# Grouped-query attention with its scores transposed, in an encoder layer on one core

## The chip, the cores and the metric

The kernel runs on one core of a Trainium2 chip. The metric is the device time of one execution in microseconds (us). Engines are named as in the profile: PE is TensorE (matrix products; PEld is its loading of weights), DVE is VectorE, ACT is ScalarE, POOL is GpSimd, SP is SyncE, which issues most DMAs. PSUM is the memory that products are written to; a bank of it holds 128 x 512 float32.

## The reference

One layer over 512 tokens of width 1024: `z = x @ w_in` is split into neighbourhood attention (8 heads of 64), grouped-query attention (8 query heads and 2 key/value heads of 64), attention into 256 memory tokens, and three gates; the branches are projected, gated, summed and normalised; then come 16 experts. What the change touches is this part:

```
q = apply_rope(rms_norm(q, q_gain), cos, sin)        # 8 query heads
k = apply_rope(rms_norm(k, k_gain), cos, sin)        # 2 key heads, 4 query heads to each
s = einsum('bkgqd,bskd->bkgqs', q, k) / sqrt(64)     # per head: 512 queries x 512 keys
p = softmax(s, axis=-1)                              # over the keys
y = einsum('bkgqs,bskd->bqkgd', p, v)
```

## The kernel before

Weights come as 74 units of 128 x 1024 over SP's queue. Each unit is split by `hi_lo` into a rounded high part (ACT) and the rest (DVE), and a product of two tensors is made as three products of such parts. A unit is split two pieces of work ahead of its use.

The program is written out by hand in the order in which each engine runs it. The mixers run as a generator that issues a piece of PE work (a gate: 24 products of 128x512; a projection, or half of a block of the neighbourhood values: 12) and yields. At each yield `run` calls one step of an attention (`at.step`) and then one background stage from `bg` (rotary of q and k). So a step of attention stands between two pieces of PE work, in one queue per engine.

Three generators concern us. `g_branch(2)` is the memory branch: 8 gates and 8 projections, 16 yields. `g_na_v` makes the neighbourhood values: 8 yields. `g_na_qk(0)` makes the first neighbourhood queries and keys: 2 yields. After them comes `g_branch(1)`, which needs the result of the grouped-query attention (`y1`).

The grouped-query attention is 16 units, each a pair of heads `hp` (0 to 3) and a block `m` of 128 queries. `S` makes the scores of two heads with queries in PSUM's partitions (two products a head: key high part and key rest, each against query high and rest stacked in 128 rows). `soft` takes the maximum per query (DVE), the exponential with its sum (ACT), and `norm` multiplies by 1/sum (DVE). One step later `T` transposes the probabilities on PE (8 products of 128x128), `tev` copies them to SBUF (one copy on DVE, one on ACT), and for two blocks together `PV` makes the values (16 float32 products with 64-column weights). `run(g_branch(2, True), 1.0, 4)` makes the first step at the fifth yield.

PSUM has eight banks here: three called `mm` for the pieces, `S0` and `S1`, `T0` and `T1`, and `Y`. `PB("S")` and `PB("T")` hand out the two banks of a kind in turn. A product into a bank waits until the bank's last reader is done.

Of the kernel before, what the change touches and what calls it, by code (L numbers as in the profile page):

```python
# [18 lines left out]
P = 128  # L19
# [28 lines left out]
HOMES = {30: "E0", 31: "A5", 32: "A6", 33: "bf", N_UNITS - 1: "A7"}  # L48
# [44 lines left out]
def layer_kernel(ctx: ExitStack, tc: tile.TileContext, xt, xn, first0, wu, bgate, rpb, gains, wrt,  # L93
# [299 lines left out]
    def rope_stages(q, zs, nh, which):  # L393
# [47 lines left out]
        def sk(g):  # L441
            if not kT:
                kT.append(heads_T(0))
            src = kT[0][g * 64:g * 64 + 64]
            for o in (0, 64):
                nc.scalar.copy(khh[o:o + 64, g], src)
            for o in (0, 64):
                nc.vector.tensor_tensor(klo[o:o + 64, g], src, khh[o:o + 64, g].bitcast(F32), op=ALU.subtract)

        def sq_(pair):  # L450
            hp = 2 * (q - 1) + pair
# [14 lines left out]
    def g_gqa():  # L466
# [4 lines left out]
                  rope=(R("VS", [P, 1024], "ropesq"), b1t[:, 1]), zr=R("B0", [P, 2, 1024], "ropeout"))  # L471
# [170 lines left out]
    class GqaUnit:  # L642
        GROUP = 2

        def __init__(self, hp, m):
            self.hp, self.m = hp, m

        def S(self):
            self.s = []
            for h in range(2):  # L650
                g = self.hp // 2
                tok = slice(self.m * P, (self.m + 1) * P)
                q = ST["qs"][g][:, 2 * (self.hp % 2) + h, tok]
                s = PB("S", f"gs{self.hp}{self.m}{h}")
                nc.tensor.matmul(s, q, ST["khh"][:, g], start=True, stop=False)
                nc.tensor.matmul(s, q, ST["klo"][:, g], start=False, stop=True)
                self.s.append(s)

        def soft(self):
            self.p = twin("P").rearrange("p (h c) -> p h c", h=2)  # L660
            self.sm = small([P, 2], "sm")
            nm = small([P, 2], "nm")
            for h in range(2):
                nc.vector.tensor_reduce(nm[:, h:h + 1], self.s[h], axis=AX.X, op=ALU.max, negate=True)  # L664
                nc.scalar.activation(self.p[:, h], self.s[h], AF.Exp, bias=nm[:, h:h + 1],  # L665
                                     accum_out=self.sm[:, h:h + 1])

        def norm(self):
            recip_norm(self.p, self.sm, lambda h: self.p[:, h])

        def T(self):
            self.t = []
            for h in range(2):
                t = PB("T", f"gt{self.hp}{self.m}{h}", (P, 4, P))
                for kc in range(4):
                    nc.tensor.transpose(t[:, kc], self.p[:, h, kc * P:(kc + 1) * P], ident)  # L676
                self.t.append(t)

        def tev(self):
            self.pt = twin("PT").rearrange("p (h k c) -> p h k c", h=2, k=4)  # L680
            nc.vector.tensor_copy(self.pt[:, 0], self.t[0])
            nc.scalar.copy(self.pt[:, 1], self.t[1])

        def PV(self, group):

            self.y = PB("Y", f"gy{self.hp}{self.m}")
            kvh = self.hp // 2
            for j, u in enumerate(group):
                for kc in range(4):
                    for h in range(2):  # L690
                        nc.tensor.matmul(self.y[h * 64:h * 64 + 64, j * P:(j + 1) * P],  # L691
                                         ST["vg"][:, kc, kvh * 64:kvh * 64 + 64], u.pt[:, h, kc],
                                         start=(kc == 0), stop=(kc == 3))

        def yev(self, group):
            yh, yl = ST["y1"]
            n = len(group) * P
# [1224 lines left out]
```

## Time and profile before

| | |
|---|---|
| median of 3 runs | 935.5 us (934.7 to 935.88) |
| the profiled execution's own time | 935.11 us |
| its span on the core | 933.3 us (1.8 us lie around it) |
| PE busy | 917.4 us (98%) |
| DVE, ACT, POOL busy | 451.6, 280.9, 72.3 us |

Busy is time in which the engine has an instruction at work. PE's products overlap, so the distance between starts tells what one costs, not its duration. A stage is read from the time by engine within it.

### The profile page before, as it was taken

How to read it: one execution, taken by the hardware profiler on the slowest of the kernel's cores; microseconds unless marked ns; L12 is line 12 of the kernel's file. 1: busy time of each engine (PE TensorE's matmuls, PEld its weight loads, DVE VectorE, ACT ScalarE, POOL GpSimd, SP SyncE). 2: the span in 40 equal slices, each digit the busy share in tenths (PEclk: the TensorE clock that was granted, in tenths of full speed). 3: DMA queues.
4: the chain of work that ended last, by engine and by line, in shares of the span. 5: the costliest groups of instructions: out<-in, count | busy, mean ns of one | idle time of the engine just before them, and what ended most of it. 6: DMA issues, size and time to landing. Idle time of an engine off the chain costs nothing.

```text
span 933.3 us, 13429 instructions
## 1 busy us (share of the span) xinstructions
PE 917.4 (98%) x5497; PEld 604.2 (65%) x5497; DVE 451.6 (48%) x859; ACT 280.9 (30%) x573; POOL 72.3 (8%) x107
## 2 busy tenths in 40 slices
PE   9999999999999999999999999999999999999996
PEld 8899988888888888888787344434343444533332
DVE  6448869875375566326545147223141323422245
ACT  6334443644344454334333011101011010301021
POOL 0000000000132230107023000000000000000001
PEclk9999999999999999999999999999999999999998
DMA  9322221222333332474878999999999999999997
GB/s 366 100 73 66 87 70 46 69 69 68 96 83 113 105 89 72 177 279 179 316 316 354 412 424 433 426 438 429 436 435 429 426 428 431 428 433 428 430 425 291
DMA packets 40012, 251.42 MB, mean 269 GB/s; under 512 B 12720, under 2 KB 13264, under 8 KB 24592
## 3 DMA queue, kind: packets, MB, share of 16 engines
q1 hardware_dynamic: 39728, 250.22, 66.9%
q8 instruction: 43, 0.70, 0.3%
q0 software_dynamic: 80, 0.26, 0.1%
q14 instruction: 17, 0.14, 0.0%
q10 hardware_dynamic: 144, 0.10, 0.0%
HBM read 247.42 MB, written 2.36 MB: 268 GB/s over the span
## 4 chain that ended last, share of the span: by engine, by line
PE 77%; DMA 16%; DVE 4%; ACT 1%; issue 0%; SPq 0%; POOLq 0%; DVEq 0%; ACTq 0%
DMA gu<-in_wst 15%; PE g L1386 7%; PE u L1386 7%; PE y L1447 6%; PE gate L306 5%; PE gate L308 4%; PE gate L307 4%; PE pr L306 2%; PE pr L307 2%; PE pr L308 2%; PE ga L1350 2%; PE gy L691 2%; PE nqk L306 2%; PE nqk L307 2%; PE nqk L308 2%; PE gt L676 1%
## 5 line engine op out<-in xcount | busy, mean ns | idle before, releaser
L1386 PE MATMUL g<-gu,xs 128*64 128x512 f32 x408 | 106.1, 598 | 0.8 <-DMA gu<-in_wst 0.7
L1386 PE MATMUL u<-gu,xs 128*64 128x512 f32 x408 | 104.9, 592 | 0.0
L1447 PE MATMUL y<-dn,hT 128*64 128x512 f32 x376 | 83.6, 593 | 0.9 <-DMA dn<-in_wst 0.8
L150 DVE TENSOR_TENSOR y<-y,y 64x512 fp32r<-64x512 f32 x28 | 19.3, 689 | 120.2 <-ACT y L149 120.2
L150 DVE TENSOR_TENSOR lo_twin<-raw_twin,whi 128x1024 fp32r<-128x1024 f32 x40 | 49.0, 1226 | 46.2 <-ACT whi L149 46.1
L149 ACT CAST y<-y 64x512 fp32r<-64x512 f32 x28 | 16.2, 580 | 174.1 <-PE y L1447 146.6
L1386 PEld LDWEIGHTS u<-gu,xs 128*64 128x64 f32 x408 | 29.4, 137 | 58.1 <-issue 57.6
L149 ACT CAST whi<-raw_twin 128x1024 fp32r<-128x1024 f32 x60 | 63.0, 1050 | 12.1 <-PE wo L1159 9.4
L1447 PEld LDWEIGHTS y<-dn,hT 128*64 128x64 f32 x376 | 27.0, 137 | 54.5 <-issue 51.5
L1386 PEld LDWEIGHTS g<-gu,xs 128*64 128x64 f32 x408 | 26.8, 137 | 46.2 <-issue 40.0
L1429 DVE COPY hT<-ht 128x512 f32<-128x512 f32 x15 | 10.4, 692 | 61.5 <-PE ht L1426 61.4
L306 PE MATMUL gate<-xha,whi 128*128 128x512 f32 x96 | 38.7, 403 | 0.0
L307 PE MATMUL gate<-xla,whi 128*128 128x512 f32 x96 | 37.4, 390 | 0.0
L306 PE MATMUL gate<-xhb,whi 128*128 128x512 f32 x96 | 37.3, 389 | 0.0
L307 PE MATMUL gate<-xlb,whi 128*128 128x512 f32 x96 | 37.3, 389 | 0.0
L712 POOL TENSOR_TENSOR bm<-bf,hm 128x256 f32<-128x256 f32 x24 | 18.9, 827 | 236.7 <-DMA bf<-in_rpb 232.9
L1535 DVE TENSOR_TENSOR acc<-acc,cb 128x512 f32<-128x512 f32 x56 | 34.0, 680 | 3.7 <-PE cb L1533 3.7
L1350 PEld LDWEIGHTS <-x 128*128 128x128 f16 (+1 forms) x576 | 29.7, 100 | 9.0 <-issue 8.7
L665 ACT ACTIVATE P_twin<-gs,nm 128x512 f32<-128x512 f32 x32 | 21.7, 684 | 42.8 <-DVE nm L664 42.8
L1410 DVE SCALAR_TENSOR_TENSOR h<-h,g 128x512 f32<-128x512 f32 x15 | 10.3, 688 | 49.5 <-ACT h L1409 49.5
L150 DVE TENSOR_TENSOR wlo<-raw_twin,whi 128x1024 fp32r<-128x1024 f32 x20 | 24.5, 1226 | 17.9 <-ACT whi L149 17.9
L308 PE MATMUL gate<-xha,lo_twin 128*128 128x512 f32 x80 | 31.2, 391 | 0.0
(489 smaller groups left out, 1998.7 us busy)
## 6 DMA issues: line engine op xcount, KB each, us to landing
gu<-in_wst SPq DMA_DIRECT2D x31, 2048.0 KB
gu<-in_wst SPq DMA_DIRECT2D x45, 1024.0 KB
raw_twin<-in_wu SPq DMA_DIRECT2D x65, 512.0 KB
dn<-in_wst SPq DMA_DIRECT2D x14, 2048.0 KB
dn<-in_wst SPq DMA_DIRECT2D x18, 1024.0 KB
gu<-in_wst SPq DMA_DIRECT2D x4, 4096.0 KB
dn<-in_wst SPq DMA_DIRECT2D x4, 4096.0 KB
gu<-in_wst SPq DMA_DIRECT2D x2, 3072.0 KB
```

The costliest lines, as they stand in the source:

```text
L149: nc.scalar.copy(hi, src)
L150: nc.vector.tensor_tensor(lo, src, hi.bitcast(F32), op=ALU.subtract)
L306: nc.tensor.matmul(acc, w_h, rh[:, k], start=(k == 0), stop=False)
L307: nc.tensor.matmul(acc, w_h, rl[:, k], start=False, stop=False)
L308: nc.tensor.matmul(acc, w_l, rh[:, k], start=False, stop=(k == nk - 1))
L665: nc.scalar.activation(self.p[:, h], self.s[h], AF.Exp, bias=nm[:, h:h + 1], accum_out=self.sm[:, h:h + 1])
L691: nc.tensor.matmul(self.y[h * 64:h * 64 + 64, j * P:(j + 1) * P], ST["vg"][:, kc, kvh * 64:kvh * 64 + 64], u.pt[:, h, kc], start=(kc == 0) ...
L712: nc.gpsimd.tensor_tensor(bm[:, h, ty].rearrange("p (b r c) -> p r b c", b=4, r=8), bf[:, h, :, 16 - 8 * ty:48 - 8 * ty].rearrange("p r (b ...
L1350: nc.tensor.matmul(g[r], part(i, m)[:, f * P + r.start:f * P + r.stop], oh[:, m], start=(i == 0 and m == 0), stop=(i == 1 and m == NT - 1))
L1386: nc.tensor.matmul(GU[e][b][hf * 64:hf * 64 + 64], xs, w[b][:, hf * 512:hf * 512 + 512], start=(k == 0), stop=(k == KD - 1))
L1447: nc.tensor.matmul(ys[o][o * 64:o * 64 + 64], hT[:, c, hf * 64:hf * 64 + 64], w[j][:, o * 512:(o + 1) * 512], start=(first and k == 0 and ...
L1535: nc.vector.tensor_tensor(a, a, cb, op=ALU.add)
```

## The change

`GqaFlow` takes the place of the 16 units. The scores are made with keys in the partitions, so that the probabilities need no transposing. The maximum per query must then be known first. `peak` makes approximate scores from the high parts alone (64 rows, queries in the partitions), and DVE takes their negative maxima. `rows` transposes them on PE into 4 rows and writes those into the moving operand of the second product, against four weight rows of ones. `scores` then gives scores less maximum, and ACT's exponential needs no bias. The sums over keys are made on POOL (`add`), then by a product with ones (`divide`); the reciprocal and the multiplication follow the values, on 128x512 per pair of heads. The query heads come in the order 0, 2, 1, 3. A step is now one pair of heads and one block of 128 keys. The start is one yield later, and steps go on at the yields of `g_na_qk(0)`; what is left runs in `gqa.drain()`. The table rows of the first neighbourhood bias are loaded at the same place as before, and POOL's additions to them follow the drain. One unit's home moves from `E0` to `VS`, and two of four DVE subtractions for the key's rest go.

```diff
+            lead = [[lambda m=m: self.peak(0, m, 0, "T"), lambda m=m: self.peak(0, m, 1, "S")] for m in range(NT)]
+            lead[0] += [lambda: self.high(0), lambda: self.high(2)]
+            self.steps += lead
+            self.steps.append([lambda: self.rows(0)])
+            todo = [(hp, kc) for hp in (0, 2, 1, 3) for kc in range(NT)]
+            for i in range(len(todo) + 3):
+                f = []
+                if 2 <= i < 6:
+                    f.append(lambda m=i - 2: self.peak(1, m, 0, "T"))
+                if i < len(todo):
+                    f.append(lambda u=todo[i], i=i: self.scores(u, i))
+                if i == 7:
+                    f.append(lambda: self.rows(1))
+                if 0 < i <= len(todo):
+                    f.append(lambda u=todo[i - 1], i=i - 1: self.values(u, i))
+                if 2 <= i < 6:
+                    f.append(lambda m=i - 2: self.peak(1, m, 1, "T"))
+                if i < len(todo):
+                    f.append(lambda u=todo[i], i=i: self.add(u, i))
...
+                if i >= 5 and (i - 5) % NT == 0 and i - 5 < len(todo):
+                    f.insert(0, lambda hp=todo[i - 5][0]: self.divide(hp))
+                self.steps.append(f)
...
+        def peak(self, j, m, h, tag):
...
+            for g in range(2):
+                o = 64 * g
+                s = PB(tag, f"gm{j}{m}{h}{g}")
+                nc.tensor.matmul(s, self.q(j + 2 * g, h)[o:o + 64, m * P:(m + 1) * P], ST["khh"][o:o + 64, g],
+                                 start=True, stop=True)
+                ss.append(s)
+            for g in range(2):
+                nc.vector.tensor_reduce(self.nm[j][:, m, g, h:h + 1], ss[g], axis=AX.X, op=ALU.max, negate=True)
...
+        def scores(self, u, i):
+            hp, kc = u
+            g, c = hp // 2, slice(kc * P, kc * P + P)
+            ss = [PB("S", f"gs{hp}{kc}{h}") for h in range(2)]
             for h in range(2):
+                nc.tensor.matmul(ss[h], ST["khh"][:, g, c], self.q(hp, h), start=True, stop=False)
             for h in range(2):
+                nc.tensor.matmul(ss[h], ST["klo"][:, g, c], self.slot(hp, h), start=False, stop=True)
+            for h in range(2):
+                nc.scalar.activation(self.pt[i % 4][:, h * S:h * S + S], ss[h], AF.Exp)
...
+                nc.gpsimd.tensor_tensor(self.acc[hp][h], old, self.pt[i % 4][:, c], op=ALU.add)
...
+            for h in range(2):
+                nc.tensor.matmul(self.y[h * 64:h * 64 + 64], v, self.pt[i % 4][:, h * S:h * S + S],
+                                 start=(kc == 0), stop=(kc == NT - 1))
+            if kc == NT - 1:
+                nc.scalar.copy(ST["gtmp"][:, S:], self.y)
+
+        def divide(self, hp):
+            rc, y = ST["gtmp"][:, :S], ST["gtmp"][:, S:]
+            sm = PB("T", f"gd{hp}")
+            for h in range(2):
+                nc.tensor.matmul(sm[h * 64:h * 64 + 64], self.ones, self.acc[hp][h], start=True, stop=True)
+            nc.vector.reciprocal(rc, sm)
+            nc.vector.tensor_tensor(y, y, rc, op=ALU.mult)
+            yh, yl = (t[:, hp] for t in ST["y1"])
+            nc.scalar.copy(yh, y)
+            nc.gpsimd.tensor_tensor(yl, y, yh.bitcast(F32), op=ALU.subtract)
...
-    run(g_branch(2, True), 1.0, 4)
-    run(g_na_v(), 1.0)
-    at.drain()
-    na_bias(0)
-    run(g_na_qk(0))
+    gqa = GqaFlow()
+    run(g_branch(2, True), 1.0, 5, gqa)
+    run(g_na_v(), 1.0, 0, gqa)
+    bf0 = na_rows(0)
+    run(g_na_qk(0), 1.0, 0, gqa)
+    gqa.drain()
+    na_bias(0, bf0)
```

Three places in the order of instructions show what stands where. In the names, `gs`, `gm`, `gy`, `gd` and `gt` are PSUM tiles (scores, approximate scores, values, sums, transposed probabilities) and the last number of a name only tells buffers apart.

The first place is behind the last projection of `g_branch(2)`, PE's order. Before, it held the scores of a unit, the values of two blocks and the transposes of the unit ahead:

```order
L655 MATMUL gs230_2008<-kk_557,qs1_560 128x512
L656 MATMUL gs230_2008<-kk_557,qs1_560 128x512
L655 MATMUL gs231_2011<-kk_557,qs1_560 128x512
L656 MATMUL gs231_2011<-kk_557,qs1_560 128x512
L691 MATMUL gy20_2014<-PT_twin_681,vgt_558 64x128 x16
L676 MATMUL gt220_2031<-ident_137,P_twin_627 128x128 x4
L676 MATMUL gt221_2036<-ident_137,P_twin_627 128x128 x4
L496 MATMUL nv0_2063<-whl30_1872,xha_101 128x512
```

Now the first `divide` stands there (`gd0`), then a pair of 64-row products, scores, values, and another such pair:

```order
L756 MATMUL gd0_1802<-gsum00_1587,ones_s_1191 64x512
L756 MATMUL gd0_1802<-gsum01_1588,ones_s_1191 64x512
L701 MATMUL gm1300_1809<-kk_557,qs0_559 128x512
L701 MATMUL gm1301_1811<-kk_557,qs1_560 128x512
L725 MATMUL gs210_1815<-qs1_560,kk_557 128x512
L725 MATMUL gs211_1816<-qs1_560,kk_557 128x512
L727 MATMUL gs210_1815<-qmax_1193,kk_557 128x512
L727 MATMUL gs211_1816<-qmax_1193,kk_557 128x512
L747 MATMUL gy2_1823<-P_twin_627,vgt_558 64x512 x2
L701 MATMUL gm1310_1826<-kk_557,qs0_559 128x512
L701 MATMUL gm1311_1828<-kk_557,qs1_560 128x512
L496 MATMUL nv0_1844<-whl30_1692,xha_101 128x512
```

Sums, 64-row products and their second round have moved in ahead of the first piece of neighbourhood values, and the transposes are gone. `gd0` lies in bank `T1`, `gm1300` in `T0`, and `gm1301` in `T1` again.

On DVE the same place reads now as follows; `gm1210` and `gm1211` are the pair of the step ahead, `pr26` is a projection:

```order
L705 TENSOR_REDUCE nmx_1666<-gm1210_1780 128x1
L705 TENSOR_REDUCE nmx_1666<-gm1211_1782 128x1
L542 SCALAR_TENSOR_TENSOR maccb_1201<-th230_1635,pr26_1750 128x512
L757 RECIPROCAL vgt_558<-gd0_1802 128x512
L758 TENSOR_TENSOR vgt_558<-vgt_558 128x512
L705 TENSOR_REDUCE nmx_1666<-gm1300_1809 128x1
L705 TENSOR_REDUCE nmx_1666<-gm1301_1811 128x1
L705 TENSOR_REDUCE nmx_1666<-gm1310_1826 128x1
L705 TENSOR_REDUCE nmx_1666<-gm1311_1828 128x1
```

The reciprocal of the sums and the product with the values stand ahead of the maxima of `gm1300` and `gm1301`; a reciprocal of 128x512 stood nowhere on DVE before.

The second place is ACT's order at the second `divide`, within `g_na_v`. `vgt` holds the undivided and then the divided values, `ygh` their rounded part, `gs110` and `gs111` are the scores of that step, `nv1` a block of neighbourhood values:

```order
L750 COPY vgt_558<-gy2_1823 128x512
L760 CAST ygh_1189<-vgt_558 128x512
L729 ACTIVATE P_twin_627<-gs110_1954 128x512
L729 ACTIVATE P_twin_627<-gs111_1955 128x512
L503 COPY v_na_1837<-nv1_1903 128x512
```

The rounding of the divided values (L760) has come to stand ahead of that step's two exponentials.

The third place is PE's order between `g_na_qk(0)` and the first gate of `g_branch(1)`. Before, nothing of the attention was left there:

```order
L306 MATMUL nqk01_2425<-xhb_102,whi35_2284 128x512
L307 MATMUL nqk01_2425<-xlb_104,whi35_2284 128x512
L308 MATMUL nqk01_2425<-xhb_102,wlo35_2285 128x512
L306 MATMUL gate10_2466<-xha_101,whi36_2388 128x512
L307 MATMUL gate10_2466<-xla_103,whi36_2388 128x512
```

Now the last step and the drain stand in between:

```order
L725 MATMUL gs330_2180<-qs1_560,kk_557 128x512
L725 MATMUL gs331_2181<-qs1_560,kk_557 128x512
L727 MATMUL gs330_2180<-qmax_1193,kk_557 128x512
L727 MATMUL gs331_2181<-qmax_1193,kk_557 128x512
L747 MATMUL gy3_2078<-PT_twin_681,vgt_558 64x512 x4
L756 MATMUL gd3_2203<-gsum30_2049,ones_s_1191 64x512
L756 MATMUL gd3_2203<-gsum31_2050,ones_s_1191 64x512
L306 MATMUL gate10_2225<-xha_101,whi36_2106 128x512
L307 MATMUL gate10_2225<-xla_103,whi36_2106 128x512
```

The last scores, two rounds of values and the sums of the last pair of heads have moved behind the last piece of `g_na_qk(0)`, with no piece of other work among them.

## Rows read from the trace of the kernel before

**Rows 1.** The page: span, busy time of the engines, the chain that ended last.

```profile
span 933.3 us, 13429 instructions
...
PE 917.4 (98%) x5497; PEld 604.2 (65%) x5497; DVE 451.6 (48%) x859; ACT 280.9 (30%) x573; POOL 72.3 (8%) x107
...
PE 77%; DMA 16%; DVE 4%; ACT 1%; issue 0%; SPq 0%; POOLq 0%; DVEq 0%; ACTq 0%
```

**Rows 2.** Windows: us, then PE, PEld, DVE, ACT, POOL busy, PEclk, DMA share, GB/s.

```profile
126.00:200.00 74.00, 73.94 (x463) 61.36 (x462) 58.13 (x110) 37.51 (x79) 0.00 (x0) 1.00 0.20 65
640.00:740.00 100.00, 100.00 (x572) 41.87 (x570) 29.73 (x62) 11.86 (x22) 0.00 (x0) 1.00 1.00 431
```

**Rows 3.** The chain in order of time, late part: start us, us, what.

```profile
529.51 6.87 PE y L1447 x32
...
761.31 36.45 DMA gu<-in_wst
```

**Rows 4.** PE by time, 110 to 128 us: start us, us, line, out<-in.

```profile
110.26 0.39 PE L306 MATMUL gate<-xha,whi 128*128 128x512 f32 x1
...
115.70 0.39 PE L306 MATMUL pr<-ymh,whi 128*128 128x512 f32 x1
...
127.07 0.39 PE L655 MATMUL gs<-kk,qs 128*128 128x512 f32 x1
```

**Rows 5.** PE by time, one step of two units.

```profile
210.93 0.39 PE L655 MATMUL gs<-kk,qs 128*128 128x512 f32 x1
...
211.93 1.97 PE L691 MATMUL gy<-PT_twin,vgt 128*64 128x128 f32 x32
213.82 1.09 PE L676 MATMUL gt<-ident,P_twin 128*128 128x128 f32 x8
214.67 0.48 PE L496 MATMUL nv<-whl,xha 128*128 128x512 f32 x1
```

**Rows 6.** PE by time: the transposes of the last query heads, and the next branch.

```profile
168.49 0.60 PE L436 MATMUL rT<-ident,ropeout 128*128 128x128 f32 x4
168.84 0.48 PE L306 MATMUL pr<-ymh,whi 128*128 128x512 f32 x1
...
250.73 0.39 PE L306 MATMUL gate<-xha,whi 128*128 128x512 f32 x1
```

**Rows 7.** PE by time, float32 products of 128-column weights.

```profile
103.88 1.06 PE L634 MATMUL my<-PT_twin,mvzs 128*128 128x128 f32 x8
104.69 0.47 PE L306 MATMUL gate<-xha,whi 128*128 128x512 f32 x1
```

**Rows 8.** Reciprocals, two lines of the kernel: duration ns min/median/max.

```profile
L588 DVE RECIPROCAL rc<-sm x24: 156/166/168, 61.9 to 226.3; 128x2 f32<-128x2 f32 x24
...
L752 DVE RECIPROCAL rc<-sm x8: 178/178/182, 266.6 to 372.3; 128x4 f32<-128x4 f32 x8
```

**Rows 9.** DVE by time, 144 to 158 us.

```profile
144.85 1.21 DVE L407 TENSOR_REDUCE rp<-ropesq 128x16 f32<-128x1024 f32 x1
...
148.27 0.68 DVE L542 SCALAR_TENSOR_TENSOR macca<-th,pr 128x512 f32<-128x512 f32 x1
...
152.46 1.22 DVE L412 TENSOR_TENSOR mvzs<-mvzs,rp 128x1024 f32<-128x1024 f32 x1
...
154.86 0.68 DVE L542 SCALAR_TENSOR_TENSOR macca<-hm,pr 128x512 f32<-128x512 f32 x1
155.46 1.22 DVE L150 TENSOR_TENSOR wlo<-raw_twin,whi 128x1024 fp32r<-128x1024 f32 x1
156.59 1.28 DVE L664 TENSOR_REDUCE nm<-gs 128x1 f32<-128x512 f32 x2
157.79 0.68 DVE L681 COPY PT_twin<-gt 128x512 f32<-128x512 f32 x1
```

**Rows 10.** Groups by line and form: ACT's exponentials, POOL's adds.

```profile
L665 ACT ACTIVATE P_twin<-gs,nm 128x512 f32<-128x512 f32 x32 | 21.7, 684 | 42.8 <-DVE nm L664 42.8
...
L546 POOL TENSOR_TENSOR macca<-macca,tm 128x512 f32<-128x512 f32 x4 | 7.0, 1749 | 35.1 <-DVE tm L545 35.1
```

More of the change, by code (lines that the diff above doesn't have):

```diff
@@ L47 @@
 N_EARLY = 12
-HOMES = {30: "E0", 31: "A5", 32: "A6", 33: "bf", N_UNITS - 1: "A7"}
+HOMES = {30: "VS", 31: "A5", 32: "A6", 33: "bf", N_UNITS - 1: "A7"}
 X_SCALE = 1024.0
@@ L446, in sk @@
                 nc.scalar.copy(khh[o:o + 64, g], src)
-            for o in (0, 64):
-                nc.vector.tensor_tensor(klo[o:o + 64, g], src, khh[o:o + 64, g].bitcast(F32), op=ALU.subtract)
+            o = 64 * g
+            nc.vector.tensor_tensor(klo[o:o + 64, g], src, khh[o:o + 64, g].bitcast(F32), op=ALU.subtract)
         def sq_(pair):
-            hp = 2 * (q - 1) + pair
+            hp = q - 1 + 2 * pair
             tp = heads_T(pair)
@@ L470, in g_gqa @@
         ST.update(khh=kk[:, 0:2], klo=kk[:, 2:4], vg=vg, qs=(R("A4", [P, 4, S], "qs0", F32R), R("A8", [P, 4, S], "qs1", F32R)),
-                  rope=(R("VS", [P, 1024], "ropesq"), b1t[:, 1]), zr=R("B0", [P, 2, 1024], "ropeout"))
+                  rope=(R("VS", [P, 1024], "ropesq"), b1t[:, 1]), gtmp=b1t[:, 1], zr=R("B0", [P, 2, 1024], "ropeout"))
         for q in range(3):
@@ L640, in yev @@
             hi_lo(yh[d], yl[d], self.y)
[L642 to L649, printed above, removed]
-            for h in range(2):
[L651 to L662, printed above, removed]
-            for h in range(2):
[L664 to L672, printed above, removed]
-            for h in range(2):
[L674 to L697, printed above, removed]
-            d = (slice(None), self.hp, slice(self.m * P, self.m * P + n))
-            hi_lo(yh[d], yl[d], self.y[:, :n])
@@ L702, in na_bias, with na_rows @@
+    def na_rows(hp):
         bf = R("bf", [P, 2, 8, 48], f"bf{hp}")
@@ L708, in na_bias @@
                     ap=[[64 * 63, 8], [63, 16], [1, 48]]))
+        return bf
+    def na_bias(hp, bf=None):
+        bf = bf or na_rows(hp)
         bm = R("A8" if hp % 2 == 0 else "B1", [P, 2, 3, 256], f"bm{hp}")
@@ L835, in layer_kernel, with run @@
     at = Attn()
-    def run(gen, every=0.0, delay=0):
+    def run(gen, every=0.0, delay=0, at=at):
         acc = -every * delay
@@ L932, in layer_kernel @@
     ST["y1"] = (R("A2", [P, 4, S], "ygh", F32R), R("A3", [P, 4, S], "ygl", F32R))
-    at.add([GqaUnit(hp, m) for hp in range(4) for m in range(NT)])
-    run(g_branch(2, True), 1.0, 4)
-    run(g_na_v(), 1.0)
-    at.drain()
-    na_bias(0)
-    run(g_na_qk(0))
+    gqa = GqaFlow()
[5 more added lines that the diff above has]
+    na_bias(0, bf0)
     at.add([NaUnit(0, i) for i in range(2)])
@@ L1846, in _prep @@
     units = mk(0) + mk(1) + mk(2) + mk(3) + mv(0) + mv(1) + qm(0) + qm(1) + qm(2) + qm(3)
-    units += [nu(w_in, 1536 + q * 256, h) for q in (2, 0, 1) for h in range(2)]
+    wq = w_in[:, 1536:2048].reshape(D, 2, 2, 128).swapaxes(1, 2).reshape(D, 512)
+    units += [nu(w_in, 2048, h) for h in range(2)]
+    units += [nu(wq, q * 256, h) for q in range(2) for h in range(2)]
     for jp in range(4):
```

64 lines of the change are left out of this document (63 added, 1 removed).

## The prediction

> **What bounds the kernel now.** I read the page first [rows 1]: PE is busy for 98% of the span, and of the chain that ended last 77% lies on PE and 16% on DMA. Next the windows [rows 2]: in 126 to 200 us, where most of the attention runs, PE is busy for 73.94 of 74 us at full clock, DVE for 58.13, and DMA at a fifth. In 640 to 740 us DMA is full. The late chain [rows 3] shows why both count: long pieces of it wait for expert weights. Those loads go out as buffers come free behind PE's work, so if the mixers end later or earlier, the stream starts later or earlier. I take a shift of the attention stage one to one to the end. The reader is to see that PE never waits long in this stage, so two things decide: what PE's own stream gains, and which waits are new on it.
>
> PE's prices come from starts that follow each other. A gate of 24 products takes 110.26 to 115.70 = 5.44 us, so 0.227 for a product of 128x512; a projection of 12 takes 2.72 [rows 4]. Of a step [rows 5], the scores of two heads take 211.93 - 210.93 = 1.0 (0.907 of products and 0.1 for the change to float32), the values of two blocks 213.82 - 211.93 = 1.89, the transposes 0.85. A first product behind float32 work lasts 0.48 instead of 0.39, so 0.1 per change [rows 4, 6]. A float32 product with 64 columns of weights leaves two records; at 512 columns 32 records take 6.87, so 0.215 each [rows 3].
>
> **The change part by part.** I split the stage at the transposes of the last query heads (168.49 us now) and end it at the first gate of the next branch (250.73) [rows 6].
>
> *Up to those transposes.* Nothing changes up to 127.07, where the first scores stood [rows 4]. Without them the transposes come there (0.35, 168.49 to 168.84 [rows 6]), then a gate (5.44 and 0.1), so the first 64-row products start at 132.96. PE alone would need from there: four steps of two pairs (0.6 each, see below), two gates, three projections, the row transposes (0.5), the first scores (0.9) and 0.5 of changes: 156.3. But VectorE's queue sets it. Up to the last rotary sums, which the transposes need, it holds 16 maxima at 0.60 (two in 156.59 to 157.79), three splits of units at 1.13 (155.46 to 156.59), the rotary reduction with its small operations (144.85 to 148.27, 3.42), two wide multiplications (152.46 to 154.86, 2.40), and ten operations at 0.60 (154.86 to 155.46): six rotary ones, two gated sums, two writes of rows, 4 rows high but as long [rows 9]. That is 9.6 + 3.4 + 3.4 + 2.4 + 6.0 = 24.8. It starts when the first product ends (0.4 after 132.96), so the transposes start at 158.3. PE waits 2.0 of that. They start 10.2 us earlier than before, with less of the attention done.
>
> *From there, PE's stream.* Before: 250.73 - 168.49 = 82.24. The other work in it is two sets of transposes (0.7), three projections (8.16), two gates (10.88), eight halves of neighbourhood values (21.76) and two blocks of queries and keys (10.88): 52.4. So the attention took 29.8. After: 15 scores at 0.907 = 13.6; 16 values, two products or four records each, at 0.86 and two changes at 0.1 = 17.0; four sums with ones at 0.96 = 3.8; eight pairs of 64-row products; one set of row transposes, 0.5.
>
> The pair of 64-row products is not in the trace. If the halves of the array run one after the other it costs 0.45; if both run at once, 0.23. The nearest rows are products that use half of the columns: 128 columns of weights take 0.81 for 8 records, 0.101 each [rows 7], while 64-column ones, in alternate halves, take 1.89 for 32, 0.059 each [rows 5]. I take at once, 0.25 and 0.1 of change: 2.8. The other end adds 0.2 x 8 = 1.6. (In the first four steps it adds little, since VectorE is late there.) Sum: 13.6 + 17.0 + 3.8 + 2.8 + 0.5 = 37.7.
>
> *The reciprocal.* Before, it stood on 2 or 4 elements: medians 166 and 178 ns [rows 8]. That is 6 ns an element, and 166 + 510 x 6 = 3.2 us for 512. The low end is the price of another DVE operation of that size, 0.60 [rows 9]; the high end takes the extremes of the two rows (156 to 182), 13 ns, so 6.8. I take 3.2. The Trainium skill ("VectorE: DVE Perf Modes", the walkthrough of the pipeline, first the fixed hardware budget) says that a reciprocal is an iterative divide with a repeat count of 8; at its 0.96 GHz that makes an estimate of 4.3 us. By the page the sum below would be 2.2 higher. Both speak against putting 128x512 on it; the old kernel did it on 128x2.
>
> *New waits on PE.* (1) At the first `divide`, behind the last projection of the branch: the sums lie in bank T1. Behind them stand `gm1300` in T0 and `gm1301` in T1, so PE waits for the reciprocal with scores and values queued behind. The wait is 3.2 + 0.3 of handing over - 0.2 for `gm1300` = 3.3. (2) At the second `divide` PE goes on, but ACT's rounding of the divided values waits for reciprocal (3.2) and multiplication (0.6), and that step's exponentials stand behind it. From the start of the sums: 0.96 + 3.2 + 0.6 + 0.68 for the rounding (as an exponential, [rows 10]) + 0.3 = 5.7, and the exponentials end at 6.4 and 7.0. PE is back for those banks after 0.96 + 0.91 + 1.06 + 2.72 + 0.1 = 5.75: waits of 0.65 and 0.45, 1.1. (3) At the third, the piece between is a 5.44 block and covers it. (4) In the drain, no piece lies between the last scores and their sums. The exponentials end 0.7 and 1.4 behind the scores, POOL's two additions (1.75 each [rows 10]) at 2.5 and 4.3; PE's two rounds of values end at 1.9. With the sums it is free at 4.8, without waiting it would be at 3.0: 1.8. Waits together: 6.2.
>
> *At nothing.* POOL's additions (24 x 1.75) come at 3.5 per step, where a step with its piece takes 4.7 or more. The maxima of the second round are taken while PE makes scores and values (2.0); if DVE is late there, up to 0.6 each. DVE loses two key subtractions, the scaling, and half of the copies, ACT the other half and the reading of sums; neither was waited for. POOL's additions for the first neighbourhood bias now stand behind the last subtraction: 4.3 + 0.5 + 3.2 + 0.6 + 0.7 + 1.75 and three additions of half the size (2.6) = 13.7 behind the last scores, while PE, with two gates first, wants them at 4.8 + 10.9 = 15.7. That cover goes if the reciprocal takes 2 us more; each further one then delays a softmax, not yet PE. On SP's queue the shift of neighbourhood values now also waits for the unit in `VS`; the second shift and the table rows behind it waited for the same products before.
>
> *Sum.* 158.3 + 52.4 + 37.7 + 6.2 = 254.6 against 250.73: 3.9 us later. 935.11 + 3.9 = 939.0 for an execution like the profiled one; the median shown is 0.4 above that execution, so I say **939.4**.
>
> **The rivals.** (A) The forecast, 939.4; its own range is 937.5 to 942. (B) The reciprocal runs like other DVE operations, 0.60: (1) shrinks to 0.7 and (2) to nothing, 3.7 less, 935.7: no change to be measured. For it: at 2 elements it costs no more than any small operation. Against: the two rows differ by 12 ns. (C) Faster: VectorE is never waited for. Its total in the stage falls (32 scalings and 16 copies go, four reciprocals come), and if it clears its queue in time, the 2.0 ahead of the transposes, (1) and (2) all fall away: 6.4 less, 933.0. It decides from where the reciprocal is under about 0.5 us and the 24.8 of its queue shrink to 22.8. Against: 16 maxima, a rotary chain and three splits stand in one queue there. (D) Slower than A: row halves take turns (1.6 more), and the reciprocal takes 8 ns an element, from 166, the median of its first row, to 182, the longest of its second [rows 8]: 4.2 us, 1.0 more at (1) and at (2). 943.0; at the steep end (6.8 us) another 5.
>
> The Trainium skill ("TensorEngine Tiling (Array Packing)", tiling modes) states that tiles of 64 rows work independently, with up to twice the rate; no run here shows it for rows, and it would leave A's 0.25.
>
> **How the numbers follow.** A 0.52, B 0.18, C 0.13, D 0.17. 0.2% (1.9 us) is about what a measurement of this kernel tells from no change. Faster than 933.6 is C's; within 933.6 to 937.4 B and the edge of A; slower the rest of A and D: 0.13, 0.21, 0.66. The range goes from 934.0, between B and C, to 945.0, which holds D without the steepest reciprocal.
>
> **What would show it.** Of the changed kernel: a reciprocal (L757) of some 3.2 us, four times; PE idle about 3.3 us ahead of the second 64-row product behind `gd0`, ended by DVE; idle of about 1 us ahead of the scores behind the second `divide`, ended by ACT; idle of some 2 us ahead of `gd3`, ended by POOL; 64-row pairs that start well under 0.2 us apart; the last rotary transposes at about 158.3 us behind a DVE wait; the first gate of the next branch near 254.6. The prediction is wrong if VectorE's queue is shorter than laid out here, if the reciprocal's price doesn't grow with its length as the two small rows say, or if the later stream of weights gives back or adds to the shift.

## The result, and the profile after

The changed kernel takes 947.99 us (median of 4 runs, 946.08 to 948.69), the kernel before 935.45 (934.7 to 935.88): 1.0134 times as long, with a 95% interval of 1.0121 to 1.0147. The direction was forecast, the size was not: 939.4, with a range up to 945.0. The profiled execution took 948.69 us, its span is 946.9; it is the slowest of the four and 13.6 us longer than the profiled one before, where the medians differ by 12.5.

The page of the changed kernel (engines with busy time, share of the span and instructions; the chain that ended last) answers to [rows 1]:

```profile
span 946.9 us, 12847 instructions
...
PE 925.2 (98%) x5233; PEld 585.8 (62%) x5233; DVE 441.3 (47%) x797; ACT 271.6 (29%) x529; POOL 119.8 (13%) x150
...
PE 76%; DMA 16%; DVE 5%; issue 1%; ACT 1%; SPq 0%; POOL 0%; POOLq 0%; DVEq 0%; ACTq 0%
```

Read alone, this page hides the loss: TensorE still is busy for 98%, and VectorE's and ScalarE's totals fell. The windows of the changed kernel show it (columns as in [rows 2]):

```profile
126.00:200.00 74.00, 68.78 (x287) 46.80 (x287) 50.31 (x74) 24.29 (x37) 10.08 (x9) 0.95 0.19 64
640.00:740.00 100.00, 100.00 (x572) 42.00 (x572) 29.71 (x62) 11.86 (x22) 0.00 (x0) 1.00 1.00 431
150.00:160.00 10.00, 7.85 (x36) 5.80 (x35) 8.12 (x13) 2.87 (x5) 0.00 (x0) 0.94 0.29 107
160.00:170.00 10.00, 10.00 (x42) 7.34 (x42) 5.52 (x8) 5.30 (x9) 2.52 (x2) 0.89 0.15 52
190.00:200.00 10.00, 6.93 (x23) 3.81 (x23) 6.69 (x7) 1.19 (x3) 1.28 (x1) 0.82 0.00 0
200.00:205.00 5.00, 5.00 (x16) 2.54 (x13) 2.58 (x4) 2.39 (x4) 3.61 (x4) 0.68 0.00 0
```

Two holes open in a stretch where TensorE hardly paused before (73.94 of 74 us busy [rows 2]), and at each of them PEclk, the granted clock as a mean of the slice, falls below 1.00 as well (products then start 0.42 us apart instead of 0.23, as at 160.37 below: half clock, 1.2 and not 2.4 GHz). TensorE by time at these two places and at the end of the stage (the bracket is the idle time ahead of the instruction and what ended it):

```profile
156.36 0.47 PE L727 MATMUL gs<-qmax,kk 128*128 128x512 f32 x1 [0.42 <-DVE qmax L718]
157.07 0.47 PE L727 MATMUL gs<-qmax,kk 128*128 128x512 f32 x1 [0.24 <-ACT qmax L716]
159.03 1.12 PE L436 MATMUL rT<-ident,ropeout 128*128 128x128 f32 x4 [1.49 <-DVE ropeout L428]
159.79 0.78 PE L306 MATMUL pr<-ymh,whi 128*128 128x512 f32 x1
160.37 0.63 PE L307 MATMUL pr<-yml,whi 128*128 128x512 f32 x1
160.79 0.63 PE L308 MATMUL pr<-ymh,wlo 128*128 128x512 f32 x1
...
193.41 0.49 PE L701 MATMUL gm<-kk,qs 64*128 64x512 f32 x1
196.96 0.79 PE L701 MATMUL gm<-kk,qs 64*128 64x512 f32 x1 [3.06 <-DVE vgt L757]
197.68 1.22 PE L725 MATMUL gs<-qs,kk 128*128 128x512 f32 x2
...
205.57 0.62 PE L725 MATMUL gs<-qs,kk 128*128 128x512 f32 x2
...
227.22 0.99 PE L725 MATMUL gs<-qs,kk 128*128 128x512 f32 x2 [0.35 <-ACT P_twin L729]
...
261.60 2.29 PE L756 MATMUL gd<-gsum,ones_s 128*64 128x512 f32 x4
263.82 0.50 PE L306 MATMUL gate<-xha,whi 128*128 128x512 f32 x1
```

The first gate of the memory branch, ahead of the stage, starts at 103.93 us here and at 104.69 before [rows 7], so this execution runs 0.76 earlier. From there to the first gate of the next branch it takes 263.82 - 103.93 = 159.89 us, before 250.73 - 104.69 = 146.04 [rows 6, 7]: 13.85 more. The span grew by 13.6, so the shift went through to the end nearly one to one, as assumed. The 13.85 come apart by these rows, and for the half clock by those of a later experiment, a copy in place of the reciprocal, where the order on TensorE is the same and the clock stayed at 1.00:

```profile
159.32 0.66 PE L436 MATMUL rT<-ident,ropeout 128*128 128x128 f32 x4 [1.49 <-DVE ropeout L428]
...
162.57 0.62 PE L725 MATMUL gs<-qs,kk 128*128 128x512 f32 x2
...
193.07 0.49 PE L701 MATMUL gm<-kk,qs 64*128 64x512 f32 x1 [0.40 <-DVE vgt L757]
...
198.95 0.62 PE L725 MATMUL gs<-qs,kk 128*128 128x512 f32 x2
```

```profile
160.00:170.00 10.00, 10.00 (x46) 7.43 (x46) 6.50 (x8) 5.60 (x10) 2.53 (x2) 1.00 0.16 52
200.00:205.00 5.00, 5.00 (x24) 3.38 (x24) 0.97 (x1) 1.22 (x3) 3.94 (x3) 1.00 0.67 211
```


- **Waits, 6.8.** The five brackets sum to 5.56. The last sums with ones take 2.22 from their start to the next instruction's, where the three others take 1.01: 1.2 of waiting for GpSimd.
- **Half clock, 4.2.** From 159.03 to the end of the projection behind the transposes (163.79) it took 4.76 us, and from 196.96 to 205.57 8.61. The same pieces took 3.25 (159.32 to 162.57) and 5.88 (193.07 to 198.95) with the copy.
- **A longer stream, 2.8**, the rest; in it is what TensorE loses beyond the idle time where its stream stops and starts again (taken apart further below).

The forecast had 8.2 us of waits, no term for the clock, and a stream 4.3 us *shorter* than before.

### The profile page after: what moved, and what is told of

It is laid out like the page before. It is cut to its first block, busy times and chain, and to the rows that moved or that the text cites. A ratio compares the mean times of both kernels' runs of the same rounds, so it can differ in the third digit from the quotient of the medians.

```text
span 946.9 us, 12847 instructions
## 1 busy us (share of the span) xinstructions
PE 925.2 (98%) x5233; PEld 585.8 (62%) x5233; DVE 441.3 (47%) x797; ACT 271.6 (29%) x529; POOL 119.8 (13%) x150
## 4 chain that ended last, share of the span: by engine, by line
PE 76%; DMA 16%; DVE 5%; issue 1%; ACT 1%; SPq 0%; POOL 0%; POOLq 0%; DVEq 0%; ACTq 0%
DMA gu<-in_wst 11%; PE g L1464 7%; PE u L1464 7%; PE y L1525 7%; PE gate L306 4%; PE gate L307 4%; PE gate L308 4%; DMA dn<-in_wst 4%; PE ga L1428 2%; PE pr L306 2%; PE pr L307 2%; PE pr L308 2%; PE nqk L306 2%; PE nqk L308 2%; PE nqk L307 2%; PE gy L747 1%
## 5 line engine op out<-in xcount | busy, mean ns | idle before, releaser
L150 DVE TENSOR_TENSOR wlo<-raw_twin,whi 128x1024 fp32r<-128x1024 f32 x20 | 24.8, 1239 | 21.3 <-ACT whi L149 21.2
L1488 DVE SCALAR_TENSOR_TENSOR h<-h,g 128x512 f32<-128x512 f32 x15 | 10.3, 687 | 49.8 <-ACT h L1487 49.8
L308 PE MATMUL gate<-xhb,lo_twin 128*128 128x512 f32 x80 | 31.1, 389 | 0.0
```

What stands on the lines that cost most here:

```text
L150: nc.vector.tensor_tensor(lo, src, hi.bitcast(F32), op=ALU.subtract)
L308: nc.tensor.matmul(acc, w_l, rh[:, k], start=False, stop=(k == nk - 1))
L1488: nc.vector.scalar_tensor_tensor(th, th, 1.0, g, op0=ALU.add, op1=ALU.mult)
```

## The experiments

Each kernel is the changed one with the edit shown. "Stage" is the profiled execution's time from the first gate of the memory branch to the first of the next branch (146.0 before, 159.9 changed). The ratio is to the kernel before, measured along with each run, with its 95% interval. Three kernels leave out work that the result needs, and only price it: the one without the second round, the one without maxima, and the copy.

| run | median us | ratio | stage us |
|---|---|---|---|
| the changed kernel | 947.99 | 1.0134 (1.0121 to 1.0147) | 159.9 |
| sums in the mm ring | 947.07 | 1.0133 (1.0116 to 1.0150) | 156.8 |
| 13 products in the wait | 945.93 | 1.0114 (1.0097 to 1.0131) | 157.3 |
| products in both waits | 944.64 | 1.0101 (1.0086 to 1.0117) | 155.9 |
| rows on ScalarE | 943.50 | 1.0100 (1.0083 to 1.0117) | 154.9 |
| mm ring, no second round | 939.82 | 1.0051 (1.0034 to 1.0067) | 151.8 |
| division last | 944.78 | 1.0103 (1.0086 to 1.0119) | 153.9 |
| division last, rows | 941.90 | 1.0066 (1.0049 to 1.0083) | 152.9 |
| the same, and the tail | 940.88 | 1.0062 (1.0046 to 1.0079) | 149.4 + 1.0 |
| the same, no maxima | 929.71 | 0.9942 (0.9925 to 0.9959) | 139.0 + 1.0 |
| the three, late rounding | 939.49 | 1.0051 (1.0037 to 1.0064) | 149.0 + 1.0 |
| copy for the reciprocal | 941.65 | 1.0075 (1.0059 to 1.0090) | 152.1 |
| the three, late reciprocal | 936.20 | 1.0011 (1.0002 to 1.0020) | 146.0 + 1.0 |

The "+ 1.0" are the last sums, which stand behind the next gate's products there.

**Sums in the mm ring.**

```diff
-            sm = PB("T", f"gd{hp}")
+            sm = PB("mm", f"gd{hp}")
```

> The divide's sums go to a bank of the mm ring; all other work stays. Theory W (the second-round maxima wait 3.1 us for the reciprocal that reads their bank, and the half clock behind that wait costs about 3.4 us more): that wait goes to under 0.5 us, the granted clock of 190 to 205 us stays at 1.00, and the time falls by 5.5 to 6.5 us, to about 942. Rival S (TensorE's own stream with its 64-row products is what is longer, and waits were only noticed there): the wait goes, other waits take its place a step later, time 946 to 948. Rival C (the clock falls for another cause than the wait): the wait goes, the clock still falls, about 945.

It gained nothing that can be measured: the time is the one that rival S named, and another wait did take the first one's place, but in the same step. TensorE in the run with the sums in the mm ring:

```profile
197.62 1.09 PE L701 MATMUL gm<-kk,qs 64*128 64x512 f32 x2 [2.31 <-DVE nmx L705]
```

VectorE ahead of it:

```profile
192.81 3.36 DVE L757 RECIPROCAL vgt<-gd 128x512 f32<-128x512 f32 x1 [2.15 <-PE gd L756]
196.27 0.69 DVE L758 TENSOR_TENSOR vgt<-vgt 128x512 f32<-128x512 f32 x1
196.88 2.56 DVE L705 TENSOR_REDUCE nmx<-gm 128x1 f32<-128x512 f32 x4
```

My account of the wait was too narrow. The bank was the first obstacle only: the step's four maxima stand behind the reciprocal in VectorE's queue, and the next 64-row products need the banks that those maxima read. So the wait came back 2.31 us long a few products later, and the clock fell behind it again (0.78 in 200 to 205 us). That its stage still reads 3.1 shorter owes 1.5 to chance: in this execution the clock did not fall at 160 to 170 us.

**Products in the waits.** These ask whether the clock falls *because* TensorE stands still.

```diff
+                if (j, m, h, g) == (1, 3, 0, 1):
+                    fill = PB("mm", "fill")
+                    for _ in range(13):
+                        nc.tensor.matmul(fill, ST["khh"][:, 0, :P], ST["khh"][:, 1], start=True, stop=True)
                 nc.tensor.matmul(s, self.q(j + 2 * g, h)[o:o + 64, m * P:(m + 1) * P], ST["khh"][o:o + 64, g],
```

> The bank of the sums stays, and 13 products of 128x512 that nothing reads are put ahead of the product that waits for it, so that TensorE works through the 3.1 us. Theory W with its second half (the clock falls because TensorE stood still): the clock stays full behind them, and the time falls by about 3.0 to 3.4 us, to about 944.8, though TensorE has 13 products more to do. Rival C (the clock falls in this stretch whatever TensorE does ahead of it): the clock is at half all the same, and the time stays at 948.

> The changed kernel with products that nothing reads in both waits: 7 ahead of the last rotary transposes and 13 ahead of the 64-row product that waits for the reciprocal. Every wait for data stays as long as it was. If the clock falls because TensorE stands still, it stays at 1.00 in every slice from 103 to 264 us, and the time is about 944.5, 1.1 to 1.6 less than with the 13 alone. If the clock falls for another cause, 160 to 170 us shows a clock under 0.95 and the time is that of the run with the 13 alone, about 946.

The second of them also puts 7 such products ahead of `rT` of the last heads' first pair. Windows of the run with 13 products, then of the run with both:

```profile
160.00:170.00 10.00, 10.00 (x41) 7.26 (x40) 4.86 (x7) 5.73 (x10) 2.52 (x2) 0.83 0.16 52
190.00:200.00 10.00, 10.00 (x41) 5.97 (x39) 7.13 (x7) 1.87 (x4) 0.91 (x1) 1.00 0.00 0
200.00:205.00 5.00, 5.00 (x22) 3.31 (x22) 4.25 (x5) 2.62 (x5) 5.00 (x5) 1.00 0.02 3
```

```profile
160.00:170.00 10.00, 9.97 (x47) 7.49 (x48) 6.02 (x8) 6.11 (x10) 2.52 (x2) 1.00 0.16 54
190.00:200.00 10.00, 10.00 (x40) 5.75 (x39) 6.60 (x7) 2.64 (x5) 2.05 (x2) 1.00 0.00 0
```

Behind the 3.06 us wait the clock fell in both profiles that left it as it was (the changed kernel, and the run with the rows on ScalarE below) and stayed at its full level in both that filled it; and a kernel with 20 products *more* ran 3.3 us faster than the changed one (944.64 against 947.99; both times as forecast within 1.2). The mean granted clock over the whole execution says the same of every run, profiled or not: 0.991 to 0.996 in the four of the changed kernel, 0.997 or 0.998 in the four with both waits filled, as in the runs of the kernel before. This shows the clock term and its cause. The medians give back 3.3 of the 4.2 us that the one profile shows; the clock does not fall alike in every execution, and behind the 1.49 us wait it fell in three of six profiles, so for that wait alone the one filled profile would prove little.

**Rows on ScalarE.**

```diff
-                    if h:
-                        nc.scalar.activation(o, r, AF.Copy, scale=one)
-                    else:
-                        nc.vector.tensor_scalar(o, r, one, None, op0=ALU.mult)
+                    nc.scalar.activation(o, r, AF.Copy, scale=one)
```

> All four writes of the rows of maxima go to ScalarE, none to VectorE, so there is no turn between the two engines. Theory L (the lead's last rotary transposes are late by the row writes that VectorE does in turn with ScalarE, 2.3 us, and the clock behind their wait costs 1.6 us): TensorE's three waits ahead of the last rotary transposes, 2.15 us, fall under 0.5, the clock of 160 to 170 stays near 1.0, time lower by 2.5 to 4 us, to about 944.7. Rival (VectorE is late by its queue from 133 us on, whoever writes the rows): the transposes begin at most 0.7 us earlier, and the time is 947 to 948.

4.5 us faster by the medians and 3.2 by the ratios (one of the four runs took 945.91), where 2.5 to 4 were forecast. In the changed kernel the four row writes took turns: VectorE, ScalarE, VectorE, ScalarE (first two fences), and the last rotary sums stood behind VectorE's second one. With all on ScalarE (third) the four writes are done by 155.7, and TensorE waits 0.31 us ahead of the last transposes:

```profile
155.47 0.74 DVE L718 TENSOR_SCALAR qmax<-gr,ident 4x512 fp32r<-4x512 f32 x1
157.03 0.74 DVE L718 TENSOR_SCALAR qmax<-gr,ident 4x512 fp32r<-4x512 f32 x1 [0.82 <-ACT qmax L716]
157.70 1.27 DVE L428 TENSOR_TENSOR ropeout<-vgt,ropesq 128x512 f32<-128x512 f32 x2
```

```profile
156.25 0.68 ACT L716 ACTIVATE qmax<-gr,ident 4x512 fp32r<-4x512 f32 x1 [8.57 <-DVE qmax L718]
157.80 0.68 ACT L716 ACTIVATE qmax<-gr,ident 4x512 fp32r<-4x512 f32 x1 [0.88 <-DVE qmax L718]
```

```profile
153.17 2.52 ACT L715 ACTIVATE qmax<-gr,ident 4x512 fp32r<-4x512 f32 x4 [5.16 <-PE gr L710]
```

ScalarE, idle for 8.57 us ahead of its first write, was held by VectorE's queue: the first write of a chain set when all others could start. Why these writes, to different places of one tile and all from one bank, take turns, no run shows.

**No second round of maxima**, in the mm ring.

```diff
-                if 2 <= i < 6:
-                    f.append(lambda m=i - 2: self.peak(1, m, 0, "T"))
...
-                if 2 <= i < 6:
-                    f.append(lambda m=i - 2: self.peak(1, m, 1, "T"))
...
+            self.nm[j] = self.nm[0]
```

> As the run with the sums in the mm ring, and without the second round's 16 products of 64 rows and their 16 maxima; the rows of the second round are written from the maxima of the first, and the exponentials are scaled by 0.01 (the softmax is left wrong by that). Against the run with the sums in the mm ring this prices the second round on TensorE: 2.8 us by my price of 0.35 us for a pair, about 4.2 if the change between 64 and 128 rows costs 0.35 us a step more, as the steps of the changed kernel's trace look. Rival V (VectorE's reductions cost the time, TensorE is only late by them): more than 4.5 us.

7.3 us less than the run with the mm ring alone: by the forecast that is rival V's (more than 4.5), but the run does not show V, nor price the pairs: without the second round's maxima nothing stands behind the reciprocal at that place, so the wait of 2.31 us and its half clock went along with the products. The price of the pairs is better read from single steps, as the next section does.

**The division behind its step**, then with the rows on ScalarE, then with the last division behind the next gate's products.

```diff
-                    f.insert(0, lambda hp=todo[i - 5][0]: self.divide(hp))
+                    f.append(lambda hp=todo[i - 5][0]: self.divide(hp))
...
-    gqa.drain()
+    gqa.step()
+    bg.append(gqa.drain)
```

> The division stands at the end of its step instead of its beginning, in the same bank as before; nothing is left out. The run with the sums in the mm ring moved the wait from the bank to the maxima that queue behind the reciprocal (2.31 us, by VectorE) and won hardly anything. Theory Q (VectorE's queue: whatever stands behind the 3.36 us reciprocal and is wanted within it stalls TensorE, and the clock at half behind the stall costs 1.5 to 2.5 us more): with the step's maxima ahead of the reciprocal both go, the time falls by 4.5 to 5.5 us, to about 943. Rival (the reciprocal only makes the next thing late, the split of the weights of nv or the next row writes): a wait of over 2 us by VectorE or ScalarE stands in 196 to 212 us instead, time 946 to 948.

> The division at the end of its step and all row writes on ScalarE. If the two stalls are apart from each other the gains add up: 4.5 us of the row writes and 4.5 to 5.5 of the division's place, time about 938. If they share a cause (VectorE's load as such), less than 7 us together, about 941. The granted clock then is 1.00 from 103 to 264 us, and the stage shows TensorE's own stream: I expect about 150 us, still 4 longer than the 146.0 of before.

> As the run before it, and the last division goes behind the first gate product group of the next branch. The 1.2 us that TensorE waits for GpSimd's last sums are covered: 1.0 to 1.2 us faster than that run, about 937. If the wait only moves to the products that use the values behind the second gate, it is no faster.

The 3.06 us wait went, but the first run won 3.2 us and not 5, because three smaller waits opened, 0.87 us by VectorE's maxima ahead of the sums, and two in `nv` for the split of its weights, 1.1 by ScalarE and 1.0 by VectorE. The rival had named that split, though it forecast hardly any gain. In the second run the clock fell to 0.66 in 200 to 205 us behind the two waits in `nv`; in the profiles of the first and third, with the same waits, it stayed. So that run missed its forecast of a clock at 1.00 and a stage of 150 us; and its time, 6.1 us less, does not decide whether the two gains add up: alone they are 4.5 and 3.2 by the medians, by the ratios 3.2 and 2.9 against 6.4 together. So theory Q has the mechanism right and misplaced its end: the reciprocal delays whatever comes next in the queue. The tail brought 1.0 by the medians but 0.4 by the ratios, within their intervals; what is shown is that the wait went, for the last sums take 1.00 us there and 2.22 in the run before it.

**No maxima at all.**

```diff
-            lead = [[lambda m=m: self.peak(0, m, 0, "T"), lambda m=m: self.peak(0, m, 1, "S")] for m in range(NT)]
+            lead = [[] for m in range(NT)]
```

and the same for the second round and both row writes.

> As the run before it, without any maxima: both rounds of 64-row products, their 32 reductions, the row transposes and the row writes are left out, and the exponentials are scaled by 0.01 so that they stay finite (the softmax is wrong by that). It prices the whole maxima pass. By my price of 0.35 us a pair and 0.5 for the rows 6.6 us less than the run before it (about 930.5); by the 0.5 us a pair that a step with two pairs shows (3.00 us against 2.01) 9 us less (about 928). A kernel without the pass is then faster than before by 5 us or more, so that the pass itself is what turns the change into a loss.

The stage is 10.3 us shorter than with the maxima (149.4 to 139.0), of which 1.2 were waits that end with them; by the medians 11.2, and that kernel, at a time between its two forecasts, beats the one before by 5.7 us. It leaves out work that the softmax needs, so it is a price and not an offer: without the pass the change would be a gain, with it no order tried here gave one. That the pass alone makes the loss, as the forecast had it, is not so: the last of the next two runs keeps the pass and loses about 1 us.

**Late rounding, late reciprocal.** Both with the three mendings and the sums in the mm ring.

```diff
+                if i >= 6 and (i - 6) % NT == 0 and i - 6 < len(todo):
+                    f.append(self.recip)
+                if i >= 7 and (i - 7) % NT == 0 and i - 7 < len(todo):
+                    f.append(lambda hp=todo[i - 7][0]: self.round(hp))
```

(The first of the two has only the rounding split off, one step behind the division; `recip` is the reciprocal and the multiplication, `round` ScalarE's rounding and GpSimd's subtraction.)

> All three mendings (division at the end of its step, rows on ScalarE, last division behind the next gate's first products), the sums in the mm ring, and the rounding of the divided values and GpSimd's subtraction one step later. Nothing is left out. In the run with the three mendings TensorE still waited 0.87 us ahead of the first sums (by VectorE's maxima) and 1.07 and 0.99 us in nv, where the split of its weights stood behind the rounding on ScalarE, which waited 6.8 us for the reciprocal. Theory Q: those 2.9 us go, the stage falls from 149.4 to 146.5 us (and the last sums behind the gate, 1.0), time about 937.5: still slower than before by 1.5 to 2.5 us, and what is left is TensorE's own stream. Rival (the wait moves to another queue again): 940 to 941.

> As the run with the late rounding, and the reciprocal with its multiplication one step later than the sums, the rounding one more. Nothing is left out. In that run the split of the weights of nv, two writes of 2.2 us on VectorE, stood behind the reciprocal, and TensorE waited 1.86 and 0.57 us for it. Theory Q: with the splits ahead of the reciprocal these 2.4 us go too, the stage falls from 149.0 to about 146.6 us (and the last sums, 1.0), time about 937.2, slower than before by 1.5 to 2.5 us with no wait over 0.4 us left on TensorE in the stage: what remains is that its stream of products is longer. Rival (some other wait of 1 us or more opens, or the splits are late for another reason than the reciprocal): 938.5 to 940.

VectorE in the run with the late rounding, and TensorE's wait:

```profile
193.61 3.35 DVE L756 RECIPROCAL vgt<-gd 128x512 f32<-128x512 f32 x1
...
198.26 4.43 DVE L150 TENSOR_TENSOR whl<-raw_twin,whl 128x1024 fp32r<-128x1024 f32 x2
```

```profile
200.53 0.50 PE L497 MATMUL nv<-whl,xhb 128*128 128x512 f32 x1 [1.86 <-DVE whl L150]
```

The same place in the run with the late reciprocal, then TensorE with its one wait and the ends of the stage, and its windows:

```profile
194.98 3.92 DVE L150 TENSOR_TENSOR whl<-raw_twin,whl 128x1024 fp32r<-128x1024 f32 x2
198.83 3.35 DVE L761 RECIPROCAL vgt<-gd 128x512 f32<-128x512 f32 x1
```

```profile
105.47 0.47 PE L306 MATMUL gate<-xha,whi 128*128 128x512 f32 x1
...
158.25 0.66 PE L436 MATMUL rT<-ident,ropeout 128*128 128x128 f32 x4 [0.31 <-DVE ropeout L428]
...
192.65 0.50 PE L705 MATMUL gm<-kk,qs 64*128 64x512 f32 x2
193.08 1.08 PE L756 MATMUL gd<-gsum,ones_s 128*64 128x512 f32 x4
...
251.43 0.49 PE L306 MATMUL gate<-xha,whi 128*128 128x512 f32 x1
```

```profile
160.00:170.00 10.00, 10.00 (x47) 7.01 (x45) 5.16 (x7) 3.89 (x6) 2.53 (x2) 1.00 0.22 60
190.00:200.00 10.00, 10.00 (x42) 5.44 (x42) 8.11 (x8) 4.05 (x6) 5.70 (x5) 1.00 0.19 56
```

The first missed its forecast (nearer to the rival: the wait moved from ScalarE's queue to VectorE's); the second came out 1.0 below its own. In it 0.31 us is the only wait that the trace shows on TensorE in the stage, the clock is at 1.00 throughout, and the stage takes 147.0 with the last sums, 0.9 more than before. It is still about 1 us slower than the kernel before (1.0011, interval 1.0002 to 1.0020), and 11.8 us better than the changed kernel with the same arithmetic: the place of a few instructions in the queues, a bank and the engine of two writes made all but about a microsecond of the loss.

**A copy for the reciprocal**, in the changed kernel.

```diff
-            nc.vector.reciprocal(rc, sm)
+            nc.vector.tensor_copy(rc, sm)
```

> The changed kernel with the reciprocal replaced by a copy of the sums (the division is wrong by that), all else in place. The reciprocal's length, 3.36 us, against about 0.6 for a copy. If the reciprocal is what holds TensorE at the first division, the wait of 3.06 us falls to about 0.4 and with it the half clock behind it: 5 to 6 us less, about 942.5. If the place in the queue counts whatever stands there, less than 2 us.

As forecast for the reciprocal's length: the wait is 0.40 us, the clock of the profile stays at 1.00, and the time falls by 6.3 us by the medians, 5.5 by the ratios. The clock stayed behind the 1.49 us wait too, which this run leaves as it was.

## Why the prediction missed

*Right.* The direction, the reciprocal's length, and where the waits stand. The reciprocal took 3.2 us in the sum; by line and form in the changed kernel (busy us, mean ns, idle time ahead):

```profile
L757 DVE RECIPROCAL vgt<-gd 128x512 f32<-128x512 f32 x4 | 13.4, 3358 | 19.5 <-PE gd L756 19.5
```

Two points 12 ns apart [rows 8] carried to 512 elements within 5%. That is 6.6 ns an element. The Trainium skill ("VectorE: DVE Perf Modes", the walkthrough of the pipeline, first the fixed hardware budget) states a repeat count of 8 for it, from which the prediction took an estimate of 4.3 us; at the 0.96 GHz of the same page's specifications the trace has 6.3 cycles an element, and the trace decides. Wait (1) was 3.06 for a forecast 3.3, (2) 0.35 for 1.1, (3) none as forecast, (4) 1.2 for 1.8 (GpSimd's two additions there took 1.25 us each and not 1.75). The transposes came at 159.03, or 159.79 with the 0.76 us by which this execution ran earlier, forecast 158.3; PE's wait there was 2.15, forecast 2.0. That these two agree is in part luck. VectorE's queue up to the last rotary sums took 26.1 us and not 24.8, 1.0 of it by the turns of the row writes, which the forecast did not have; and PE alone was 0.9 later than forecast. With the rows on ScalarE the wait was 0.31, where the forecast's queue without its two writes (1.2) would have left 0.8. The shift went through to the end. B and C fell with the reciprocal and with VectorE's queue.

*The first step that failed: "From there, PE's stream"*, 7.1 us of the 9.95 by which 13.85 exceeds the forecast 3.9. It was made of prices for undisturbed blocks (0.227 a product, 2.72 for 12), and so the attention's share before, 29.8, a difference, was too large. Before's own trace has the truer price; TensorE there, the scores behind the piece of `nv` that starts at 214.67 [rows 5]:

```profile
217.53 0.39 PE L655 MATMUL gs<-kk,qs 128*128 128x512 f32 x1
```

2.86 us for 12 products, and the fifteen pieces of other work behind 168.49 take 53.9 and not 52.4. In the run with the late reciprocal, which shows the stream without waits, they take 55.0 (+2.6 against the sum), the 15 scores about 1.00 each and not 0.907 (+1.3), the 16 values 1.01 or 0.91 and not 1.06 (-1.0), the eight pairs 0.43 each and 0.11 more on four scores behind them (+1.1), the sums and rows +0.1, and PE alone reaches the last transposes at 157.2 and not 156.3 (+0.9): 5.0. The other 2.1 stand in the changed kernel and not in that one. About 1.5 are at three waits, 0.5 each beyond the idle time, where the stream stops and starts again: in the run with the copy, at full clock, the pair around 193.07 takes 1.31 us (192.19 to 193.50) with 0.40 of it idle, and 0.43 elsewhere. The rest, about 0.6, comes from the sums standing ahead of the scores: at the third division, where nothing waits, a block of `nv`, sums, scores, values and the next block take 8.94 us, and 8.62 in the order of the late reciprocal.

The pair's size went wrong by its changes, not by its halves. TensorE in the run with three mendings, lead:

```profile
132.61 0.73 PE L701 MATMUL gm<-kk,qs 64*128 64x512 f32 x4
133.27 0.50 PE L306 MATMUL pr<-ymh,whi 128*128 128x512 f32 x1
```

Two pairs take 0.66, one takes 0.43 (193.08 - 192.65 in the run with the late reciprocal), so the second pair costs 0.23, the price of *one* product: both halves of the array run at once. The Trainium skill says so ("TensorEngine Tiling (Array Packing)", tiling modes), and the trace agrees. But going into 64-row tiles costs 0.2 (0.43 less 0.23) and out of them 0.1 (the 0.11 on the scores), where the sum had 0.1 together.

*The second: no term for the clock*, 4.2 us. "PE is busy for 73.94 of 74 us at full clock" was read from the windows [rows 2] and then kept, in a stage that I filled with 8 us of waits. The fill runs show that the two belong together: with both waits filled the clock stayed full, and behind the long one it fell each time that it was left.

*The third, small:* "Waits together" with the 2.0 ahead of them, 6.8 and not 8.2. Rival D had the row halves in turn and a longer reciprocal, neither of which came; its number was nearest for other reasons. Together -4.3 + 7.1 for the stream, 4.2 for the clock and 8.2 - 1.4 of waits give the measured 13.8.

## What to carry over

When a long operation enters a queue, the question is not which wait it causes but what stands behind it for its whole length: three of the mendings (another bank, the division behind its step, the late rounding) each moved the wait to the next thing in VectorE's or ScalarE's queue, and only issuing the reciprocal behind everything wanted soon ended it. A stall of some microseconds on a TensorE that was always busy should get a second price, for the clock behind it. Price a stream by pieces as they stand between the others, with their changes of tile shape; a remainder got by subtraction takes every error of the rest.

## What the runs showed of the hardware

- The granted clock fell behind waits as short as 1.5 us (in three of six profiles of the same wait) and behind two of 1.0 us (one of four profiles), stayed up behind 1.86 and 0.57 us in the run with the late rounding, and stayed up when the same time was filled with products whose results nothing reads. Why it falls at one and not at another of the same waits, the traces do not show.
- VectorE's two splits of 128x1024 in the run with the late rounding took 2.25 us each, where such splits take 1.24 on average in the changed kernel. The starts and ends fit turns with GpSimd: an addition ends at about 199.3, the first split at 200.46, the next addition (2.27 instead of 1.28) at 201.61, the second split at 202.69, and GpSimd's subtraction at 203.83, each 1.1 us behind the other engine's.
- A four-row write of 512 columns costs 0.74 us on VectorE and 0.68 on ScalarE, as much as 128 rows do (0.69 for the multiplication behind the reciprocal). Four in a row on ScalarE take 2.52 us; handed back and forth between the engines they took 3.0.
